# Two chunks' scores in one visit, and both halves of a group's decay and rate projections in one visit

## The chip, the cores and the metric

The kernel runs on one core of a Trainium2 chip. The metric is the device time of one execution in microseconds (us), the median of several runs. TensorE (PE) does the matmuls, VectorE (DVE) and ScalarE (ACT) the elementwise work and the emptying of PSUM banks, GpSimd (POOL) a few fills, and SyncE (SP) starts the transfers.

## The reference, cut to what matters

One layer of a hybrid decoder over 256 tokens with a model width of 2048:

```
z   = rms_norm(x) @ w_in                        # pool part, r, k, v, decay, rate, gate parts
w   = -softplus(-(w0 + tanh(zw) @ w_up)) - 0.5  # decay = exp(-exp(w))
a   = sigmoid(a0 + za @ a_up)                   # rate
kk  = normalise(k * k_k); k = k * (1 + (a - 1) * k_a)
y   = wkv7_scan(r, decay, k, v, -kk, kk * a)    # per head: S = S*w + (S a) b + v k ; y = S r
x   = x + concat(pool_mixer(z), group_norm(y) * gate) @ w_out
x   = x + squared_relu(rms_norm(x) @ w_ffn_up) @ w_ffn_down
x   = x + sigmoid(rms_norm(x) @ w_ple_gate) * (p @ w_ple_proj) ; final rms_norm
```

The scan runs in 16 heads of size 64. The kernel does it in chunks of 64 tokens: within a chunk the step-by-step recurrence becomes products of small matrices, and only the state goes from chunk to chunk.

## The kernel before, in words

**Products in split precision.** Weights come from memory by SP in pieces of 128 x 1024 (`load_raw`). Each is split into a rounded half and a rest: ACT makes `wh` (line 151, two instructions) and DVE makes `wl` (line 152). Three buffers each hold raw, wh and wl. A product is three matmuls: wh by the high half of the activations, wh by the low half, wl by the high half. `gemm_cols` (lines 164 to 166, weights stationary, 256 columns) makes zk, zr and zv; `gemm_toks` (lines 173 to 175, 512 columns) makes the pool part zp and the output products. Both are generators: after each three matmuls they yield their estimated time, 0.36 or 0.68 us.

**The order on PE** is written out by hand: PE keeps the order of the program text. The long products stand in `queue` and are the filler. `fill(us)` takes steps from the queue until their yields sum up to us, and `finish(gen)` takes all that is left of one product. Between the fills stand the short, dependent steps of the recurrence, here called visits. The order on DVE, ACT and SP is set by a scheduler from priorities: the weight splits and several small steps have a high one. A second generator, `inverse`, is advanced beside the filler by `pace`: one step for each 1.65 us of filler in group 0, 0.95 in group 1.

**Two groups of eight heads** (gi = 0, 1) go through the same visits, one after the other. `rwkv_lora(gi)` (line 460) computes decay and rate of 512 channels: the decay rows stand in partitions 0 to 63, the rate rows in 64 to 127, so that two matmuls on 64 rows each can stand beside each other. It goes in two halves of two blocks, with `fill(0.7)` between; a half takes two PSUM banks, lw and la, and ACT empties them with a sigmoid each (lines 463, 464). `rwkv_k` normalises k: eight tiny matmuls into kkn (line 493), a square root, a transpose into rnT, a split into rnp (ACT line 156, DVE line 157), and the broadcast rnb (lines 512, 513), whose second matmul reads the DVE half. `rwkv_r` finishes AR. `rwkv_scores(gi)` (line 572) multiplies BK by AR for four chunks: a chunk takes two banks, one for the even and one for the odd head of each pair, eight matmuls in two passes each, and DVE empties each bank with the causal mask into SC (line 579). Ahead of every chunk but the first stands `fill(2.6)`. `rwkv_sources` scales BK on ACT (line 591) and transposes it (bkt, line 597). `inverse` inverts the triangular blocks: copies of SC into tmp (line 612), a transpose into AT (line 616), 31 pairs of DVE operations on X and tmp (lines 621, 625), and transposes of X into T1G (line 630) and tmp (line 634). `rwkv_merge` (gm, line 649; qm, line 656), `rwkv_values` (vt, bsum) and `rwkv_core` use the results.

**Banks.** Eight PSUM banks: four (`mm`) for the long products and four (`rw`) for all visits. `rw_bank` takes the next one; who takes a bank waits until its last reader is through. Which of the four it is comes out when the program is built.

The order of calls: lora, k and r of group 0, its scores, its inverse beside sources 0, lora 1, k 1 and r 1, then values 0, scores 1, merge 0, and so on. The filler is zk and zr of group 0, zv 0 around the scores of group 0, zk and zr of group 1, zp 0 around the scores of group 1, then zv 1, zp 1 and the output products.

Of the kernel before, what the change touches and what calls it, by code (L numbers as in the profile page):

```python
# [12 lines left out]
ALU = mybir.AluOpType  # L13
# [3 lines left out]
T = 256  # L17
# [23 lines left out]
def trunk(  # L41
# [19 lines left out]
    nc = tc.nc  # L61
# [11 lines left out]
    def rw_bank(name):  # L73
        return psr.tile([128, 512], F32, tag="rw", name=name)
# [5 lines left out]
    def col(name, j):  # L80
        o = PARAM_COLS[name] + j
        return par_sb[:, o : o + 1]
# [142 lines left out]
    def advance():  # L225
        try:
            us = next(queue[0])
            pace(us)
            return us
        except StopIteration:  # L230
            queue.pop(0)
            return 0.0

    def fill(us):

        while us > 0 and queue:
            us -= advance()
# [44 lines left out]
    def e4(tag):  # L282
        return rp.tile([128, 4, T], F32, tag=tag, name=f"{tag}_t")
# [55 lines left out]
    for kg, (tg, n) in enumerate((("tE", 1), ("tF", 2), ("zk", 3), ("zr", 3), ("zv", 3), ("BK", 2), ("BKt", 2))):  # L339
# [13 lines left out]
        if kg == 4:  # L353
            for tt in range(2):
                for i, q in enumerate((2, 3)):
                    nc.tensor.matmul(
                        sbank[:, tt : tt + 1], sums[q][:, 0, tt * 128 : (tt + 1) * 128], ones[:, 0:1],
                        start=i == 0 and tt == 0, stop=i == 1, skip_group_check=True,
# [27 lines left out]
    zwa, zg, zg2 = zf[:, 0], zf[:, 1], zf[0:64, 2]  # L386
# [61 lines left out]
    def rwkv_lora(gi):  # L448
        raw = rp.tile([128, 512], F32, tag="tF", name=f"wa{gi}")
        nc.sync.dma_start(raw, wa_up[:, gi * 512 : (gi + 1) * 512])  # L450
        st = {}
        sg, aa = e4("tA"), e4("tD")
        for half in range(2):
            if half:
                fill(0.7)
            bw, ba = rw_bank("lw"), rw_bank("la")
            for bk, r in ((bw, slice(0, 64)), (ba, slice(64, 128))):
                for j in range(2):
                    pc_ = slice((half * 2 + j) * 128, (half * 2 + j + 1) * 128)
                    nc.tensor.matmul(bk[:, j * T : (j + 1) * T], raw[r, pc_], zwa[r], start=j == 0, stop=True, skip_group_check=True)  # L460
            for j in range(2):
                p = half * 2 + j
                nc.scalar.activation(sg[:, p, :], bw[:, j * T : (j + 1) * T], AF.Sigmoid, bias=col("w0", 4 * gi + p))
                nc.scalar.activation(aa[:, p, :], ba[:, j * T : (j + 1) * T], AF.Sigmoid, bias=col("a0", 4 * gi + p))
        cs = e4("tB")
        for p in range(4):
            nc.vector.tensor_tensor_scan(cs[:, p, :], rmask, sg[:, p, :], 0.0, op0=ALU.mult, op1=ALU.add)
        P, EI = e4("tA"), e4("tC")
        nc.scalar.activation(P, cs, AF.Exp, scale=-WDEC)
        nc.scalar.activation(EI, cs, AF.Exp, scale=WDEC)  # L470
        pc = rp.tile([128, 4, 4], F32, tag="pc", bufs=2, name=f"pc{gi}")
        nc.vector.tensor_copy(pc, P.rearrange("p a (c t) -> p a c t", t=64)[:, :, :, 63])
        st.update(P=P, EI=EI, aa=aa, pc=pc)
        return st
# [84 lines left out]
    def rwkv_scores(gi, st, cs=(0, 1, 2, 3)):  # L559

        AR, BK = st["AR"], st["BK"]
        if 0 in cs:
            st["SC"] = rp.tile([128, 2, 4, 8, 64], F32, tag="SC", bufs=2, name=f"SC{gi}")
        SC = st["SC"]
        cm = cmask.rearrange("s (k t) -> s k t", k=2)
        for c in cs:
            if c:
                fill(2.6)
            bks = [rw_bank(f"sc{e}") for e in range(2)]
            for p in range(4):  # L570
                for e in range(2):
                    nc.tensor.matmul(
                        bks[e][:, p * 128 : (p + 1) * 128],
                        BK[e * 64 : (e + 1) * 64, p, c].rearrange("p i t -> p (i t)"),
                        AR[e * 64 : (e + 1) * 64, p, c].rearrange("p i t -> p (i t)"),
                        start=True, stop=True,
                    )
            for e in range(2):
                nc.vector.tensor_tensor(
                    SC[:, :, c].rearrange("s k (p e) t -> s k p e t", e=2)[:, :, :, e, :],  # L580
                    bks[e].rearrange("s (p k t) -> s k p t", k=2, t=64),
                    cm.unsqueeze(2).to_broadcast([128, 2, 4, 64]), op=ALU.mult,
                )

    def rwkv_sources(gi, st):

# [304 lines left out]
    wag_out()  # L891
    fill(14.0)
    st0 = rwkv_lora(0)
    finish(p_zk0)
    make_bands()
    rwkv_k(0, st0, zk0[0])
    finish(p_zr0)
    rwkv_r(0, st0, zr0[0])
    fill(7.0)
    rwkv_scores(0, st0)  # L900
    beside += [inverse(0, st0), 1.65, 0.0]
    rwkv_sources(0, st0)
    finish(p_zv0)
    st1 = rwkv_lora(1)
    finish(p_zk1)
    rwkv_k(1, st1, zk1[0])
# [4 lines left out]
    rwkv_values(0, st0, zv0[0])  # L911
    fill(7.0)
    rwkv_scores(1, st1)
    rwkv_merge(0, st0)
    beside += [inverse(1, st1), 0.95, 0.0]
# [439 lines left out]
```

## Time and profile before

| | |
|---|---|
| Median of 3 runs | 1205.03 us (1204.11 to 1207.36) |
| Span of the profiled execution, first to last instruction | 1198.9 us |
| Median less that span (what lies around it, and the difference between executions) | 6.1 us |
| TensorE busy | 1179.6 us |
| Mean granted TensorE clock | 0.996 |

The profile is of one execution. Of this execution the page gives the span alone, so a sum is made against 1198.9 us and carried over to the median. A row of the timeline gives start, duration, engine, line, operation, output and inputs; xN means that N equal records are merged. Matmuls overlap, so the distance between two starts, and not the duration, is what one costs. A matmul on plain float32 leaves two records (two passes), one on the split halves leaves one; transposes leave one.

### The profile page before, as it was taken

How to read it: one execution, taken by the hardware profiler on the slowest of the kernel's cores; microseconds unless marked ns; L12 is line 12 of the kernel's file. 1: busy time of each engine (PE TensorE's matmuls, PEld its weight loads, DVE VectorE, ACT ScalarE, POOL GpSimd, SP SyncE). 2: the span in 40 equal slices, each digit the busy share in tenths (PEclk: the TensorE clock that was granted, in tenths of full speed). 3: DMA queues.
4: the chain of work that ended last, by engine and by line, in shares of the span. 5: the costliest groups of instructions: out<-in, count | busy, mean ns of one | idle time of the engine just before them, and what ended most of it. 6: DMA issues, size and time to landing. Idle time of an engine off the chain costs nothing.

```text
span 1198.9 us, 18442 instructions
## 1 busy us (share of the span) xinstructions
PE 1179.6 (98%) x7076; PEld 1013.6 (85%) x7076; DVE 868.1 (72%) x1150; ACT 687.7 (57%) x1260; POOL 15.4 (1%) x65
## 2 busy tenths in 40 slices
PE   8999999999999999999999999999999999999996
PEld 6999988988888888888888788888888888778886
DVE  8687987854556667666888878666667888887552
ACT  6857565665545556555555555555555655668544
POOL 4000000000000000000000000000000000000000
PEclk9999999999999999999999999999999999999999
DMA  7463542354355565666665666665565655776631
GB/s 250 151 202 110 173 155 95 121 186 142 116 177 169 185 185 191 192 193 189 194 203 197 197 197 203 195 187 189 192 193 178 211 198 191 290 234 219 194 121 71
DMA packets 60328, 216.88 MB, mean 181 GB/s; under 512 B 6736, under 2 KB 7120, under 8 KB 59856
## 3 DMA queue, kind: packets, MB, share of 16 engines
q1 hardware_dynamic: 59952, 215.19, 55.1%
q8 instruction: 55, 0.90, 0.3%
q10 hardware_dynamic: 288, 0.52, 0.1%
q14 instruction: 33, 0.27, 0.1%
HBM read 213.59 MB, written 2.10 MB: 180 GB/s over the span
## 4 chain that ended last, share of the span: by engine, by line
PE 81%; DMA 6%; DVE 6%; ACT 4%; issue 2%; SPq 0%; ACTq 0%; DVEq 0%
PE u_w L986 20%; PE u_w L990 10%; DMA raw_d<-in_w_ffn_down_dram 5%; PE d_b L1101 4%; PE d_b L1100 4%; PE d_b L1102 4%; PE gt_b L173 2%; PE gt_b L175 2%; PE gt_b L174 2%; PE zv_b L164 1%; PE zp_b L173 1%; PE wag_b L333 1%; PE zv_b L165 1%; PE zv_b L166 1%; PE zp_b L175 1%
## 5 line engine op out<-in xcount | busy, mean ns | idle before, releaser
L986 PE MATMUL u_w<-h,wh_u 128*128 128x512 f32 x1024 | 355.4, 393 | 0.0
L990 PE MATMUL u_w<-h,wl_u 128*128 128x256 f32 x1024 | 285.5, 279 | 0.0
L151 ACT ACTIVATE wh_u<-raw_u 128x512 fp32r<-128x512 f32 x256 | 147.6, 624 | 162.9 <-PE u_w L986 82.0
L152 DVE TENSOR_TENSOR wl_u<-raw_u,wh_u 128x1024 fp32r<-128x1024 f32 x128 | 156.6, 1224 | 112.1 <-ACT wh_u L151 112.1
L986 PEld LDWEIGHTS u_w<-h,wh_u 128*128 128x128 f32 x1024 | 191.8, 187 | 43.2
L990 PEld LDWEIGHTS u_w<-h,wl_u 128*128 128x128 f32 x1024 | 193.1, 189 | 0.1
L152 DVE TENSOR_TENSOR wl_gt<-raw_gt,wh_gt 128x1024 fp32r<-128x1024 f32 x24 | 29.4, 1225 | 23.9 <-ACT wh_gt L151 23.9
L151 ACT ACTIVATE wh_gt<-raw_gt 128x512 fp32r<-128x512 f32 x48 | 27.8, 631 | 23.0 <-PE gt_b L175 20.4
L1140 DVE TENSOR_TENSOR td<-raw_d 128x512 f32<-128x512 f32 x22 | 15.2, 692 | 33.9 <-DMA raw_d<-in_w_ffn_down_dram 33.9
L164 PE MATMUL zv_b<-hTh,wh_zv 128*128 128x256 f32 x128 | 37.7, 294 | 0.0
L173 PE MATMUL gt_b<-wh_gt,h 128*128 128x512 f32 x96 | 37.5, 390 | 0.0
L164 PE MATMUL zr_b<-hTh,wh_zr 128*128 128x256 f32 x128 | 37.5, 293 | 0.0
L175 PE MATMUL gt_b<-wh_gt,h 128*128 128x512 f32 x96 | 37.4, 389 | 0.0
L174 PE MATMUL gt_b<-wl_gt,h 128*128 128x512 f32 x96 | 37.4, 389 | 0.0
L166 PE MATMUL zr_b<-hTh,wl_zr 128*128 128x256 f32 x128 | 37.2, 290 | 0.1
L164 PE MATMUL zk_b<-hTh,wh_zk 128*128 128x256 f32 x128 | 37.0, 289 | 0.0
L165 PE MATMUL zr_b<-hTl,wh_zr 128*128 128x256 f32 x128 | 36.9, 288 | 0.0
L165 PE MATMUL zk_b<-hTl,wh_zk 128*128 128x256 f32 x128 | 36.3, 284 | 0.5 <-DVE hTl L157 0.5
L166 PE MATMUL zk_b<-hTh,wl_zk 128*128 128x256 f32 x128 | 36.3, 284 | 0.2 <-DVE wl_zk L152 0.2
L166 PE MATMUL zv_b<-hTh,wl_zv 128*128 128x256 f32 x128 | 36.2, 283 | 0.0
L165 PE MATMUL zv_b<-hTl,wh_zv 128*128 128x256 f32 x128 | 36.2, 283 | 0.0
L156 ACT ACTIVATE wad<-raw_d 128x512 fp32r<-128x512 f32 x22 | 13.9, 632 | 36.6 <-DMA raw_d<-in_w_ffn_down_dram 34.5
(804 smaller groups left out, 3081.4 us busy)
## 6 DMA issues: line engine op xcount, KB each, us to landing
raw_u<-in_w_ffn_up_dram SPq DMA_DIRECT2D x128, 512.0 KB, 3.5
raw_d<-in_w_ffn_down_dram SPq DMA_DIRECT2D x128, 512.0 KB, 4.2
raw_gt<-in_w_ple_gate_dram SPq DMA_DIRECT2D x24, 512.0 KB, 3.5
raw_zk<-in_w_in_dram SPq DMA_DIRECT2D x16, 512.0 KB, 3.3
raw_zr<-in_w_in_dram SPq DMA_DIRECT2D x16, 512.0 KB, 3.3
raw_zv<-in_w_in_dram SPq DMA_DIRECT2D x16, 512.0 KB, 3.3
raw_zp<-in_w_in_dram SPq DMA_DIRECT2D x16, 512.0 KB, 3.2
raw_o<-in_w_out_dram SPq DMA_DIRECT2D x16, 512.0 KB, 3.5
```

Source lines behind the costliest of these rows:

```text
L151: nc.scalar.activation(wh[:, a * 512 : (a + 1) * 512], raw[:, a * 512 : (a + 1) * 512], AF.Copy)
L152: nc.vector.tensor_tensor(wl, raw, wh.bitcast(F32), op=ALU.subtract)
L164: nc.tensor.matmul(o, w_h, ah, start=first and ct % 2 == 0, stop=False, skip_group_check=True)
L165: nc.tensor.matmul(o, w_h, al, start=False, stop=False, skip_group_check=True)
L166: nc.tensor.matmul(o, w_l, ah, start=False, stop=last, skip_group_check=True)
L173: nc.tensor.matmul(o, a_h, wh[:, 0:n], start=first, stop=False)
L174: nc.tensor.matmul(o, a_h, wl[:, 0:n], start=False, stop=False)
L175: nc.tensor.matmul(o, a_l, wh[:, 0:n], start=False, stop=last)
L986: nc.tensor.matmul(bank[:, ct, :].rearrange("p (s t) -> p s t", s=2), wh[:, c], hl, start=k == 0, stop=False, skip_group_check=True,)
L990: nc.tensor.matmul(bank[:, ct, 0:T], wl[:, c], hl[:, 0, :], start=False, stop=k == 15, skip_group_check=True)
L1100: nc.tensor.matmul(banks[n], ah, wh, start=first, stop=False)
L1101: nc.tensor.matmul(banks[n], ah, wl, start=False, stop=False)
```

## The change

In `rwkv_lora` both halves take their banks at once and all eight matmuls stand together, decay and rate alternating; the fill between the halves is gone. In `rwkv_scores` two chunks take four banks, their sixteen matmuls stand together, and the four evictions follow. Of the three fills of 2.6 one fill of 5.2 is left. Lines from there on have a number that is two to three higher.

```diff
         sg, aa = e4("tA"), e4("tD")
+        banks = [(rw_bank("lw"), rw_bank("la")) for _ in range(2)]
+        for p in range(4):
+            for bk, r in zip(banks[p // 2], (slice(0, 64), slice(64, 128))):
+                nc.tensor.matmul(
+                    bk[:, p % 2 * T : (p % 2 + 1) * T], raw[r, p * 128 : (p + 1) * 128], zwa[r],
+                    start=p % 2 == 0, stop=True, skip_group_check=True,
+                )
         for half in range(2):
-            if half:
-                fill(0.7)
-            bw, ba = rw_bank("lw"), rw_bank("la")
-            for bk, r in ((bw, slice(0, 64)), (ba, slice(64, 128))):
-                for j in range(2):
-                    pc_ = slice((half * 2 + j) * 128, (half * 2 + j + 1) * 128)
-                    nc.tensor.matmul(bk[:, j * T : (j + 1) * T], raw[r, pc_], zwa[r], start=j == 0, stop=True, skip_group_check=True)
+            bw, ba = banks[half]
             for j in range(2):
...
-        for c in cs:
-            if c:
-                fill(2.6)
-            bks = [rw_bank(f"sc{e}") for e in range(2)]
-            for p in range(4):
+        for c0 in cs[::2]:
+            if c0:
+                fill(5.2)
+            two = [(c, [rw_bank(f"sc{e}") for e in range(2)]) for c in (c0, c0 + 1)]
+            for c, bks in two:
+                for p in range(4):
+                    for e in range(2):
+                        nc.tensor.matmul(
+                            bks[e][:, p * 128 : (p + 1) * 128],
+                            BK[e * 64 : (e + 1) * 64, p, c].rearrange("p i t -> p (i t)"),
+                            AR[e * 64 : (e + 1) * 64, p, c].rearrange("p i t -> p (i t)"),
+                            start=True, stop=True,
+                        )
+            for c, bks in two:
                 for e in range(2):
-                    nc.tensor.matmul(
-                        bks[e][:, p * 128 : (p + 1) * 128],
-                        BK[e * 64 : (e + 1) * 64, p, c].rearrange("p i t -> p (i t)"),
-                        AR[e * 64 : (e + 1) * 64, p, c].rearrange("p i t -> p (i t)"),
-                        start=True, stop=True,
+                    nc.vector.tensor_tensor(
+                        SC[:, :, c].rearrange("s k (p e) t -> s k p e t", e=2)[:, :, :, e, :],
+                        bks[e].rearrange("s (p k t) -> s k p t", k=2, t=64),
+                        cm.unsqueeze(2).to_broadcast([128, 2, 4, 64]), op=ALU.mult,
                     )
-            for e in range(2):
-                nc.vector.tensor_tensor(
-                    SC[:, :, c].rearrange("s k (p e) t -> s k p e t", e=2)[:, :, :, e, :],
-                    bks[e].rearrange("s (p k t) -> s k p t", k=2, t=64),
-                    cm.unsqueeze(2).to_broadcast([128, 2, 4, 64]), op=ALU.mult,
-                )
```

## The prediction on record

> **What bounds the kernel now.** I read the page first, then the busy time by stretches, then the timeline of each engine around the edited visits.
>
> ```profile
> span 1198.9 us, 18442 instructions
> ...
> PE 1179.6 (98%) x7076; PEld 1013.6 (85%) x7076; DVE 868.1 (72%) x1150; ACT 687.7 (57%) x1260; POOL 15.4 (1%) x65
> ...
> PE 81%; DMA 6%; DVE 6%; ACT 4%; issue 2%; SPq 0%; ACTq 0%; DVEq 0%
> ```
>
> TensorE (PE) is busy for 98% of the span and has 81% of the chain that ended last, so PE time saved or lost is time of the kernel, unless another engine sets the pace where it falls. The edits lie between 42 and 190 us. The stretches there (us, then busy time and count of PE, PEld, DVE, ACT, POOL, granted clock, DMA share, GB/s):
>
> ```profile
> 80.00:106.00 26.00, 26.00 (x241) 24.98 (x240) 18.71 (x22) 15.54 (x32) 0.00 (x0) 1.00 0.41 144
> 106.00:118.00 12.00, 12.00 (x97) 11.01 (x96) 11.48 (x30) 10.49 (x20) 0.00 (x0) 1.00 0.29 99
> 118.00:165.00 47.00, 46.65 (x366) 45.21 (x364) 45.97 (x84) 27.87 (x53) 1.10 (x2) 0.96 0.49 168
> 165.00:190.00 25.00, 25.00 (x206) 20.04 (x205) 15.98 (x22) 14.20 (x30) 0.00 (x0) 1.00 0.38 126
> ```
>
> PE is full in all four, but from 106 to 165 us VectorE (DVE) is full too (11.48 of 12, 45.97 of 47): there a PE that comes earlier meets halves of weights that DVE hasn't made yet. The waits of PE between 38 and 420 us are two, both on DVE, none on a DMA:
>
> ```profile
> PE h2t L1007 <- DVE x L945: 0.4, 1, 0.4
> PE zk_b L166 <- DVE wl_zk L152: 0.2, 1, 0.2
> ```
>
> So the loads that change place in SP's list (raw_zp1_3 and raw_zp1_4 behind pool weights and gate rows, the second pool load ahead of x and raw_o1a_4) cost nothing: no PE wait there ends with a transfer. If that cover went, a PE step would wait for the one load that was passed.
>
> **What a visit costs.** Score visit and rate visit of group 0, on PE (start, us):
>
> ```profile
> 85.08 0.28 PE L166 MATMUL zv_b<-hTh,wl_zv 128*128 128x256 f32 x1
> 85.29 1.16 PE L572 MATMUL sc<-AR,BK 64*128 64x128 f32 x16
> 86.38 0.38 PE L164 MATMUL zv_b<-hTh,wh_zv 128*128 128x256 f32 x1
> 86.60 0.28 PE L165 MATMUL zv_b<-hTl,wh_zv 128*128 128x256 f32 x1
> ```
>
> ```profile
> 42.77 0.28 PE L166 MATMUL zk_b<-hTh,wl_zk 128*128 128x256 f32 x1
> 42.98 0.48 PE L460 MATMUL lw<-zf,wa 64*128 64x256 f32 x1
> ...
> 43.30 0.38 PE L460 MATMUL lw<-zf,wa 64*128 64x256 f32 x1
> ...
> 43.52 0.38 PE L460 MATMUL lw<-zf,wa 64*128 64x256 f32 x1
> ...
> 44.05 0.39 PE L164 MATMUL zk_b<-hTh,wh_zk 128*128 128x256 f32 x1
> 44.28 0.28 PE L165 MATMUL zk_b<-hTl,wh_zk 128*128 128x256 f32 x1
> ```
>
> Filling matmuls follow each other every 0.12 us. The 16 passes of a score visit run as 8 pairs (two row halves), one each (1.16 - 0.27) / 8 = 0.11 us. From 85.08 to 86.60 are 1.52 us; less two filler steps (0.24) and 8 pairs (0.88) 0.40 us are left for going in and out. The rate visit gives the same: 44.28 - 42.77 = 1.51, less 0.24, less 4 pairs of 0.22 (43.30 to 43.52): 0.39. lw and la already run side by side before the change (the la rows stand 0.01 us behind), so their new order adds nothing.
>
> **What goes.** Each call of rwkv_lora loses one visit, each of rwkv_scores two: six visits x 0.40 = **2.4 us** less, 1.6 of it ahead of the second scores, 0.8 in them. Nothing else goes: matmuls, evictions and splits are the same in number. The filler isn't kept inside the scores: three fills of 2.6 were 24 steps (zv) and 12 (zp), one of 5.2 is 15 and 8. The other 9 and 4 steps run later under finish; as work nothing is lost, but the second half of the scores stands 9 x 0.36 + 0.8 = 4.0 us earlier in group 0.
>
> At the first rate visit the fourth bank is freed by this DVE row, at 43.98:
>
> ```profile
> 43.50 0.48 DVE L298 SCALAR_TENSOR_TENSOR zf<-wagT,par_sb,zf 128x255 f32<-128x255 f32 x1
> ```
>
> The new visit reaches it at 42.98 + 0.32 + 3 x 0.22 = 43.96: at most 0.1 us, taken as 0.
>
> **What comes: banks.** In the built program the four score tiles of group 0 get banks 4, 7, 6, 5, and no one waits. Group 0's second visit comes 15 x 0.36 = 5.4 us after the first and needs four evictions, 2 x 1.29 = 2.6 us. ACT scales eight pieces of BK in a row instead of four ahead of the next weight's copy; PE asks for that weight only behind the second visit, so this costs nothing while the fill lasts. In group 1 bank 5 is left out: the first visit gets 4, 7, 6, 4 and the second 7, 6, 4, 7. So in each the odd bank of the second chunk is the even bank of the first, and PE must wait inside the visit until DVE has evicted it. Before, the same reuse fell behind a fill. The rows of group 1:
>
> ```profile
> 172.83 1.16 PE L572 MATMUL sc<-AR,BK 64*128 64x128 f32 x16
> ```
>
> ```profile
> 172.13 1.23 DVE L152 TENSOR_TENSOR wl_zp<-raw_zp,wh_zp 128x1024 fp32r<-128x1024 f32 x1 [1.21 <-ACT wh_zp L151]
> 174.03 1.29 DVE L579 TENSOR_TENSOR SC<-sc,cmask 128x512 f32<-128x512 f32 x2 [0.67 <-PE sc L572]
> ```
>
> DVE starts 1.20 us after the visit and evicts two banks in 1.29, the first in some 0.69: ready 1.9 us after the start. PE would want it after 8 pairs and the way in, 1.0 us. That is 0.95 us, and some 0.15 for a pair that is torn: 1.1 us, twice: **+2.2 us**. Behind PE's waiting matmul stand the rest of the chunk, the filler and, the second time, the merge's matmuls; the merge's banks come free while PE finishes the chunk. Bounds: 0.8 (torn pair free) to 2.3 (the split of 1.23 us right ahead of the eviction) a wait. I take 1.1, since DVE is idle for 0.67 us ahead of the eviction, as the row says.
>
> [...] It holds 0.08 of the forecast's chance below, at 1207.6, inside its bounds.
>
> **What comes: DVE's order.** The scheduler sets a new list on DVE and ACT:
>
> ```profile
> 98.96 1.29 DVE L579 TENSOR_TENSOR SC<-sc,cmask 128x512 f32<-128x512 f32 x2 [0.23 <-PE sc L572]
> 102.42 1.23 DVE L152 TENSOR_TENSOR wl_zk<-raw_zk,wh_zk 128x1024 fp32r<-128x1024 f32 x1 [2.17 <-ACT wh_zk L151]
> 103.56 2.16 DVE L616 STREAM_TRANSPOSE AT<-tmp 64x1024 f32<-64x1024 f32 x1
> ...
> 145.84 2.09 DVE L630 STREAM_TRANSPOSE T1G<-X 32x512 f32<-32x512 f32 x2
> 147.78 0.40 DVE L157 TENSOR_TENSOR rnp<-rnT,rnp 8x256 fp32r<-8x256 f32 x1
> 148.10 1.20 DVE L152 TENSOR_TENSOR wl_zr<-raw_zr,wh_zr 128x1024 fp32r<-128x1024 f32 x1
> 149.23 1.15 DVE L634 STREAM_TRANSPOSE tmp<-X 64x512 f32<-64x512 f32 x1
> ```
>
> The inverse of group 0 begins at AT, 3.3 us after the last eviction (100.25). That eviction comes 3.7 us earlier (4.0, less 0.3 that four in a row queue), so AT starts near 99.9, with the same ACT steps between. From AT to the end of rnp, the small split that PE needs for rnb, DVE has 44.6 us without a gap (103.56 to 148.18). In the new list that stretch holds four more operations: one wl_zk that stood ahead of AT, one wl_zr and both transposes of X into tmp, 1.1 + 1.1 + 2 x 1.1 = 4.4 us. So rnp ends at 99.9 + 44.6 + 4.4 = 148.9, where it ended at 148.18. PE used it here:
>
> ```profile
> 148.60 0.38 PE L512 MATMUL rnb<-rnp,hsel 8*128 8x256 f32 x1
> 148.82 0.28 PE L513 MATMUL rnb<-rnp,hsel 8*128 8x256 f32 x1
> ```
>
> With 1.6 us saved PE would come at 147.2 and waits until 148.95 or so. **The 1.6 us are lost again, with 0.2 on top: +1.8.** The waits on wl_zk (122.14 in the row below) lie inside this bound and aren't added. After rnb DVE is ahead of before, as the moved work is done, and the rest is PE's. Bounds: 0 (PE keeps its gain) to 4.4 (AT isn't earlier).
>
> Sum: -2.4 + 2.2 + 1.8 = **+1.6 us**, on the profiled 1198.9 us of span: 1200.5. The median of the runs shown, 1205.03, holds 6.1 us more than that span; I carry the difference over: **1206.6**. About 0.3% (3.6 us) is what a measurement of this kernel can tell from no change.
>
> **The rivals.**
>
> *The gain arrives (faster).* The page's clock is below full here, and PE waits twice:
>
> ```profile
> 122.14 0.38 PE L166 MATMUL zk_b<-hTh,wl_zk 128*128 128x256 f32 x1 [0.23 <-DVE wl_zk L152]
> ```
>
> ```profile
> 142.00:144.00 2.00, 2.00 (x12) 2.00 (x11) 1.90 (x9) 1.95 (x5) 0.00 (x0) 0.52 0.66 240
> 144.00:146.00 2.00, 2.00 (x13) 2.00 (x13) 1.90 (x6) 0.07 (x1) 0.00 (x0) 0.63 0.84 242
> ```
>
> If the earlier inverse lets DVE run ahead, 0.4 us of wait and the dip, 2 x 0.48 + 2 x 0.37 = 1.7 us, go as well, and if DVE empties the banks in time the waits go too: -2.4 - 0.4 - 1.7 = -4.5: 1200.5. Against it: 44.6 us of DVE without a gap.
>
> *Only the banks cost:* -2.4 + 2.2: 1204.8.
>
> *DVE's list comes late (slower).* Place: rnp ahead of rnb. The list is 4.4 us longer and is saved by AT's earlier start alone. If ACT's copies into tmp, now on both sides of a weight split, keep AT later than some 102 us, rnp ends past 151 and PE loses 2.1 us or more besides: price up to 3.7, 1206.6 + 2.1 to 3.7 = 1208.7 to 1210.3, taken as 1209.3.
>
> *Another dip of the clock.* The dip above follows a stretch of tiny matmuls (kkn) and a wait. The new waits make more of these: 1.7 us each, 1208.3. [...]
>
> That the change doesn't do what it says holds for the filler, as counted above; it is in the sum.
>
> **How the numbers follow.** Forecast 0.33 (1205.0 to 1208.2 by its bounds, within 0.3% but for 0.03); only banks 0.10, within; gain arrives 0.17, 0.15 of it faster; late list 0.30, all slower; another dip 0.10, 0.07 of it slower. Faster 0.15, within 0.3% 0.45, slower 0.40. The range leaves out most of the gain's case and the far end of the late list: 1202.0 to 1210.3.
>
> **What would show it.** PE steps of over 0.9 us between sc rows in both visits near 173 and 180 us, none in group 0's; the four evictions in a row; AT near 100; rnp ending near 149 behind two tmp transposes, with PE waiting at the second rnb matmul; PE at scores of group 1 not earlier than 172.8. Wrong, if PE stands at kkn or rnb over 1.5 us later than before, or if group 1's visits run through, or if the clock dips at another place.

## The result, and the profile after

| | before | after |
|---|---|---|
| Median, 22 runs each | 1204.4 us | 1208.88 us |
| Span of the profiled execution | 1198.9 us | 1203.4 us |
| Lost to the granted clock: (1 - mean clock) x span, mean over the runs | 4.1 to 4.3 us (three sets of 35 runs, those of the experiments) | 7.1 us (22 runs) |

The ratio is 1.0029, 95% interval 1.0018 to 1.0040: 3.5 us slower (2.2 to 4.8), about the 0.3% that the prediction took as the least that can be told from no change. (The medians lie 4.5 us apart and the means 3.8, both inside the interval.) The predicted time of 1206.6 is 2.3 us below the median, which lies in the range of 1202.0 to 1210.3; the predicted difference of +1.6 us lies below the interval. In a second set of runs the changed kernel came out at 1.0046 (1.0030 to 1.0061). One run of the variant g1_single, at 1964.1 us and a granted clock of 0.556, is left out of all its figures below.

The page of the changed kernel, its span, the busy time of the engines and the chain that ended last:

```profile
span 1203.4 us, 18444 instructions
...
PE 1182.7 (98%) x7076; PEld 1017.2 (85%) x7076; DVE 869.0 (72%) x1150; ACT 688.9 (57%) x1260; POOL 15.2 (1%) x65
...
PE 87%; DVE 5%; DMA 4%; ACT 3%; issue 1%; SPq 0%; DVEq 0%; ACTq 0%
```

PE has as many matmuls as before and 3.1 us more of busy time, so the loss isn't idle time alone. The waits of PE from 38 to 420 us (line, tile, what it waited for: us in total, times, longest) show the idle part:

```profile
PE sc L574 <- DVE SC L582: 1.1, 2, 0.6
PE zk_b L166 <- DVE wl_zk L152: 1.0, 2, 0.6
PE kkn L494 <- ACT tF_t L482: 0.4, 1, 0.4
PE h2t L1010 <- DVE x L948: 0.4, 1, 0.4
PE rnb L514 <- DVE rnp L157: 0.3, 1, 0.3
```

Before, this list held h2t with 0.4 and wl_zk with 0.2. Every new wait stands at or behind an edited visit; but the 0.3 at rnb, near 65 us, is also in two executions below whose code up to there is the old one (g1_scores_alone and g1_again, 0.3 each), so it can't be put down to the change. The two score visits of group 1 on PE's timeline:

```profile
173.46 1.38 PE L574 MATMUL sc<-AR,BK 64*128 64x128 f32 x18
175.39 1.16 PE L574 MATMUL sc<-AR,BK 64*128 64x128 f32 x14 [0.56 <-DVE SC L582]
...
182.14 1.38 PE L574 MATMUL sc<-AR,BK 64*128 64x128 f32 x18
184.08 1.16 PE L574 MATMUL sc<-AR,BK 64*128 64x128 f32 x14 [0.56 <-DVE SC L582]
185.16 2.38 PE L652 MATMUL gm<-T1G,SC 32*32 32x32 f32 x64
```

Each is torn after its first chunk and one pair: 3.09 us from 173.46 to the end of the second row. Group 0's evictions and the start of its inverse on DVE:

```profile
87.04 2.48 DVE L582 TENSOR_TENSOR SC<-sc,cmask 128x512 f32<-128x512 f32 x4 [0.18 <-PE sc L574]
...
94.66 2.48 DVE L582 TENSOR_TENSOR SC<-sc,cmask 128x512 f32<-128x512 f32 x4
99.30 1.23 DVE L152 TENSOR_TENSOR wl_zv<-raw_zv,wh_zv 128x1024 fp32r<-128x1024 f32 x1 [2.17 <-ACT wh_zv L151]
100.44 2.17 DVE L619 STREAM_TRANSPOSE AT<-tmp 64x1024 f32<-64x1024 f32 x1
```

Four evictions in a row, no wait of PE there, and AT at 100.4 where it was 103.6. The same list ahead of rnb, then PE at it:

```profile
144.62 1.05 DVE L637 STREAM_TRANSPOSE tmp<-X 64x512 f32<-64x512 f32 x1
145.57 1.17 DVE L152 TENSOR_TENSOR wl_zr<-raw_zr,wh_zr 128x1024 fp32r<-128x1024 f32 x1
146.67 1.22 DVE L637 STREAM_TRANSPOSE tmp<-X 64x512 f32<-64x512 f32 x1
147.80 1.17 DVE L152 TENSOR_TENSOR wl_zr<-raw_zr,wh_zr 128x1024 fp32r<-128x1024 f32 x1
148.90 0.40 DVE L157 TENSOR_TENSOR rnp<-rnT,rnp 8x256 fp32r<-8x256 f32 x1
```

```profile
149.17 0.38 PE L513 MATMUL rnb<-rnp,hsel 8*128 8x256 f32 x1
149.39 0.34 PE L514 MATMUL rnb<-rnp,hsel 8*128 8x256 f32 x1
```

Both transposes into tmp now stand ahead of rnp, which ends at 149.3. The last new thing is the clock, in busy time by stretches (the granted clock is the third number from the right):

```profile
142.00:144.00 2.00, 2.00 (x13) 2.00 (x13) 1.97 (x5) 1.69 (x5) 0.00 (x0) 0.66 0.64 238
144.00:146.00 2.00, 2.00 (x12) 2.00 (x11) 2.00 (x4) 0.48 (x1) 0.00 (x0) 0.50 0.46 174
186.00:188.00 2.00, 2.00 (x45) 1.91 (x42) 0.36 (x1) 1.00 (x2) 0.00 (x0) 0.75 0.03 8
188.00:190.00 2.00, 2.00 (x6) 1.54 (x5) 0.00 (x0) 1.98 (x4) 0.00 (x0) 0.50 0.00 0
```

The dip at 142 was there before; the one from 187.0 to 190.4, right behind the second torn visit, is new. In it PE counts as busy throughout (2.00 of 2.00), so this dip shows in the clock column alone. (Every trace of this study, before and after, also ends at half the clock, for its last 4 to 7 us, 6.0 in the trace after; such ends aren't called dips here.)

**Where the time goes, in this pair of executions.** Start of the first instruction of a visit on PE, and the difference less the 0.30 us that the execution after already stands behind at 19 us:

| | before | after | difference less 0.30 | between the rows |
|---|---|---|---|---|
| group 0: lw | 42.98 | 43.28 | 0.00 | |
| kkn | 56.94 | 57.08 | -0.16 | one rate visit less: -0.16 |
| scores | 85.29 | 85.84 | +0.25 | waits near 59 and 65 us: +0.41 |
| group 1: lw | 107.56 | 107.33 | -0.53 | two score visits less: -0.78 |
| values (vt) | 161.72 | 162.34 | +0.32 | one rate visit less, -0.41; waits at wl_zk and kkn: +1.26 |
| merge (gm) | 186.04 | 185.16 | -1.18, or +1.58 for equal work | 12 filler matmuls fewer by then, 2.76; two visits less and two waits: +1.26 |
| h2t | 355.23 | 358.45 | +2.92 | the second dip: +1.34 |

For the other traces below a place is told in the same way: the difference from the trace of before, less what the trace stands behind it at 19 us.

From h2t on the two traces can't be compared, since PE itself runs the same matmuls of the FFN's up product at two speeds, at a granted clock of 1.00. The matmuls of that product from 400 to 570 us (duration: least, median, most), before and after:

```profile
L986 PE MATMUL u_w<-h,wh_u x491: 390/391/392, 399.7 to 569.6; 128*128 128x512 f32 x164
```

```profile
L989 PE MATMUL u_w<-h,wh_u x482: 395/398/404, 399.8 to 569.7; 128*128 128x512 f32 x161
```

The speed doesn't go with the kernel. Of the fourteen traces of this study six have 391 ns here, the changed kernel's second one (changed_again) among them, and eight have 398, the kernel before with one buffer moved among them; the trace after has 391 ns itself from 744 to 900 us. The whole up product takes 524.3 us in the trace of before, 526.9 in the trace after, and up to 532.2 in the others. So these 2.7 us of the difference between the spans are no effect of the change; the 2.9 us up to h2t fit the 3.5 of the ratio.

### The profile page after: what moved, and what is told of

Read it like the earlier page. It is cut to its first block, busy times and chain, and to the rows that moved or that the text cites. A ratio compares the mean times of both kernels' runs of the same rounds, so it can differ in the third digit from the quotient of the medians.

```text
span 1203.4 us, 18444 instructions
## 1 busy us (share of the span) xinstructions
PE 1182.7 (98%) x7076; PEld 1017.2 (85%) x7076; DVE 869.0 (72%) x1150; ACT 688.9 (57%) x1260; POOL 15.2 (1%) x65
## 4 chain that ended last, share of the span: by engine, by line
PE 87%; DVE 5%; DMA 4%; ACT 3%; issue 1%; SPq 0%; DVEq 0%; ACTq 0%
PE u_w L989 20%; PE u_w L993 10%; PE d_b L1104 6%; PE d_b L1105 6%; PE d_b L1103 6%; PE gt_b L173 2%; PE gt_b L175 2%; PE gt_b L174 2%; DMA raw_d<-in_w_ffn_down_dram 1%; PE zp_b L173 1%; PE zv_b L164 1%; DMA graw<-in_w_ple_gate_dram 1%; PE d_w L1104 1%; PE d_w L1105 1%; PE d_w L1103 1%; PE zv_b L166 1%
## 5 line engine op out<-in xcount | busy, mean ns | idle before, releaser
L152 DVE TENSOR_TENSOR wl_zp<-raw_zp,wh_zp 128x1024 fp32r<-128x1024 f32 x16 | 19.5, 1221 | 16.1 <-ACT wh_zp L151 16.1
```

The lines of the kernel that those rows point to most:

```text
L152: nc.vector.tensor_tensor(wl, raw, wh.bitcast(F32), op=ALU.subtract)
```

## The experiments

The theory: visits saved and DVE's list cancel, the banks cost 2.1 us, and the torn visits bring a second dip of the clock, which the sum had left out. Time is read from the ratio to the kernel before, run beside the variant on the same chip (three chips in all), places from the trace, and the clock from all runs of a kernel:

| kernel | ratio (95%) | lost to the clock, us |
|---|---|---|
| before | 1 | 4.3, 4.1, 4.2 |
| changed | 1.0029 (1.0018 to 1.0040) | 7.1 |
| changed_again | 1.0046 (1.0030 to 1.0061) | 7.5 |
| bank_freed | 0.9994 (0.9980 to 1.0008) | 5.1 |
| g1_scores_alone | 1.0003 (0.9988 to 1.0017) | 5.4 |
| g1_again (the same kernel) | 1.0024 (1.0003 to 1.0045) | 5.3 |
| g1_freed | 1.0010 (0.9994 to 1.0025) | 3.9 |
| g0_scores_alone | 1.0006 (0.9987 to 1.0024) | 4.6 |
| lora_alone | 0.9984 (0.9968 to 1.0000) | 4.6 |
| t1g_moved_in_before | 0.9995 (0.9980 to 1.0011) | 3.7 |
| g1_single | 1.0022 (1.0001 to 1.0043) | 5.0 |
| gap_before_merge | 1.0038 (1.0019 to 1.0057) | 5.4 |
| freed_later | 1.0008 (0.9993 to 1.0023) | 5.1 |
| no_pairs | 1.0010 (0.9993 to 1.0028) | 5.2 |

The means in the last column are uncertain by 0.2 to 0.7 us (their standard error; 0.1 to 0.2 for before), so that 3.7 and 4.6 hardly differ. One dip of 3.41 us counts as 1.71 in the last column and costs 1.5: in a dip a filler matmul takes 0.213 us instead of 0.12 (zr in the trace of before, 142.19 to 145.18 us against 138.31 to 139.15), so 16 are done in place of 28.

**The bank.** Bank 5 is left out of group 1's scores since it holds the first values product until ACT copies it into UV (line 673); UV takes the buffer of T1G, which the merge has to read first. ACT's row in the trace after shows that this copy waits for the merge's second product:

```profile
193.40 1.21 ACT L673 ACTIVATE UV<-vt 64x512 f32<-64x512 f32 x2 [0.49 <-PE qm L659]
```

It comes behind all scores. With T1G elsewhere the bank is free in time:

```diff
-        T1G = rp.tile([64, 32, 32], F32, tag=tags[0], name=f"T1G{gi}")
+        T1G = rp.tile([64, 32, 32], F32, tag=tags[0] if gi else "q3", name=f"T1G{gi}")
```

> The changed kernel, in which the matrix T1G of group 0 lies in another buffer, so that the first values bank (bank 5) is emptied before the scores of group 1 and these get four different banks (5, 4, 7, 6 in each visit). Theory: the two score visits of group 1 shrink from 3.02 us to 2.0 (-2.1 us), and with the waits goes the second dip of the clock that the changed kernel shows at 187.0 to 190.4 us (-1.5): 3.6 us less than the changed kernel, within 0.5 us of the kernel before. Rival: the dip belongs to the small matmuls of the merge behind the visits: it stays, and 2.1 us less than the changed kernel, some 1.4 us more than before. Second rival: VectorE's four evictions themselves set the pace of the visits (the merge then waits for its banks): less than 1 us is gained.

The score visits and the merge on PE, and the stretches around them:

```profile
173.49 2.06 PE L574 MATMUL sc<-AR,BK 64*128 64x128 f32 x32
...
181.14 2.06 PE L574 MATMUL sc<-AR,BK 64*128 64x128 f32 x32
183.13 2.21 PE L652 MATMUL gm<-T1G,SC 32*32 32x32 f32 x64
```

```profile
165.00:190.00 25.00, 25.00 (x262) 20.65 (x261) 16.26 (x22) 15.55 (x32) 0.00 (x0) 1.00 0.32 106
...
186.00:188.00 2.00, 2.00 (x22) 1.43 (x22) 0.00 (x0) 2.00 (x3) 0.00 (x0) 1.00 0.00 0
188.00:190.00 2.00, 2.00 (x56) 1.92 (x54) 1.89 (x2) 1.95 (x4) 0.00 (x0) 1.00 0.00 0
```

Each visit runs through in 2.06 us instead of 3.09: 2 x 1.03 us, the predicted 2.2. The clock is 1.00 in all these stretches; the dip at 142 us is in this trace too. At h2t PE is 3.7 us earlier than in the changed kernel (-0.78 against +2.92), and the whole loss is gone: 0.9994. Over the runs the clock loses 5.1 us in place of 7.1 to 7.5, and 4.3 in the kernel before. The theory holds; the rival (a dip that stays) and the second rival (evictions as the bound) fall. That the buffer by itself brings nothing is shown by the kernel before with the same edit:

> The kernel before, in which T1G of group 0 lies in the other buffer too, nothing else. It tells whether the other buffer by itself brings something. Theory: nothing, since no score visit of the kernel before waits for a bank: TensorE at the merge within 0.2 us of the kernel before. Rival: the earlier emptying of the values bank helps by itself, and 1 us or more is gained at the merge.

0.9995. Its values and merge stand 1.05 us earlier than in the trace of before, but 0.5 of it is there at group 0's scores, far ahead of the buffer's use, and this execution had no dip at 142 us; from the values to the merge nothing changes. This trace brought something else. The two longest of PE's waits from 38 to 420 us:

```profile
PE rym L707 <- DVE sbd L747: 0.8, 1, 0.8
PE rnb L513 <- DVE rnp L157: 0.7, 1, 0.7
```

Without a dip ahead of it, PE waits 0.7 us for rnp even with nothing joined; g1_scores_alone, g1_again and g1_freed, whose code is the old one up to there, show the same 0.7. The trace of before hid this: its dip at 142 us held PE back. (Why rym, behind the merge, waits 0.8 us here isn't known; at h2t PE stands at +0.07.)

**Group 1's scores alone, with and without the bank.** The kernel before with `cs` taken in twos for gi = 1 only:

```diff
-        for c in cs:
-            if c:
-                fill(2.6)
+        n = 2 if gi else 1
+        for c0 in cs[::n]:
+            if c0:
+                fill(2.6 * n)
```

> The kernel before, in which the scores of group 1 alone go in double visits, with the one fill of 5.2 us; group 0 and the projections are as before. Theory: this part alone brings the loss: -0.8 us of two visits, +2.1 us of waiting inside the double visits, +1.5 us of a second dip of the clock near 187 us: +2.8 us against the kernel before by the trace behind the merge. Rival: the dip comes only with the other parts: +1.3 us.

> Once more the kernel before with double visits for the scores of group 1 alone, beside its variant with the freed bank on one chip. Theory: from the values to the merge 1.25 us lost, the clock loses some 1 to 2.5 us more than in the kernel before: 0.2% slower. Rival, by the first reading of this kernel (1.0003): the loss isn't there unless the other parts are.

> The kernel before with double visits for the scores of group 1 alone, and with T1G of group 0 in the other buffer, so that these visits get four banks. Theory: two visits less and no wait: 0.8 us won from the values to the merge, the clock as in the kernel before; all other work unchanged: 0.05 to 0.1% faster than before, at the edge of what shows in the median. Rival: the four evictions in a row make the merge late, and nothing is won.

From the values to the merge PE loses 1.26 us in both executions of the first kernel (with the 2.76 us of filler that it has done less by then), as in the changed one. Behind it the first execution has a dip of four times 3.41 us, from 188.2 to 201.9, the second one dip at 190:

```profile
188.00:190.00 2.00, 2.00 (x32) 1.84 (x30) 0.00 (x0) 1.15 (x2) 0.00 (x0) 0.55 0.00 0
190.00:192.00 2.00, 2.00 (x6) 1.55 (x5) 0.00 (x0) 1.98 (x4) 0.00 (x0) 0.50 0.00 0
...
196.00:200.00 4.00, 4.00 (x27) 3.35 (x26) 1.64 (x8) 1.81 (x4) 0.00 (x0) 0.50 0.05 16
```

So the dip belongs to this part, and how long it lasts changes from one execution to the next. Over the runs it costs 1.1 us of clock more than before, less than the single traces let one expect. In time the two readings, 1.0003 and 1.0024, overlap, and the expected 0.2% lies just outside the first. With the bank freed the same visits last 2.06 us each, 0.81 us are won from the values to the merge, as expected, and the clock loses 3.9 us, as before. In the median 0.8 us can't be seen (1.0010, 0.9994 to 1.0025).

**The other parts alone.** Group 0's scores in double visits (n = 1 if gi else 2), and the joined projections with the scores as before:

> The kernel before, in which the scores of group 0 alone go in double visits. Theory: 0.8 us are saved at the scores (86 to 101 us), no wait inside the visits; the inverse starts some 3 us earlier, two transposes into tmp go ahead of rnp, and waits on wl_zk, kkn or rnp between 117 and 149 us give back the gain: TensorE at the values (161.7 us before) within 0.3 us of before. Rival: VectorE is early enough and the 0.8 us arrive at the values.

> The kernel before, in which only the projections of decay and rate go in one visit a group. Theory: in group 0 0.2 us are saved and lost again on rnp near 65 us; in group 1 0.4 us are saved at 108 us and lost again on wl_zk, kkn or rnp, since VectorE is full from 106 to 148 us: TensorE at the values within 0.3 us of before. Rival: the 0.6 us stay saved.

The main waits of PE in the first, then in the second:

```profile
PE rnb L513 <- DVE rnp L157: 1.7, 2, 1.4
PE zk_b L166 <- DVE wl_zk L152: 0.6, 1, 0.6
...
PE kkn L493 <- ACT tF_t L481: 0.4, 1, 0.4
```

```profile
PE rnb L514 <- DVE rnp L157: 0.9, 2, 0.7
PE zk_b L166 <- DVE wl_zk L152: 0.5, 1, 0.5
```

The visits are saved (-0.78 us between the scores and group 1's lw in the first; -0.34 at group 0's kkn in the second) and lost again. At the values PE is 1.76 and 0.98 us later than in the trace of before, more than the 0.3 expected. But in both the dip comes at 152 us, behind rnb, where it was ahead of rnb in before. The fair comparison is with the four executions whose code is the old one up to the values (two with T1G in the other buffer): t1g_moved_in_before and g1_scores_alone, without a dip there, and g1_again and g1_freed, with the dip at 152 us. From group 1's lw to the values, with the 1.5 us of their own dip taken off, these four change by -0.54 to -0.57 us against the trace of before, group 0's scores alone by +0.89 and the projections alone by -0.57. So group 0's scores lose 1.4 us there, their own 0.8 and 0.6 to 0.7 more, and the projections lose just the 0.4 that their visit saved. The rivals (the gain stays) fall in the trace; the ratios, 1.0006 and 0.9984, are too wide to add to it, and the second would even allow the gain.

**Is it DVE's list?** The changed kernel without the 31 pairs of group 0's inverse:

```diff
-        for k in range(31):
+        for k in range(31 if gi else 0):
```

> The changed kernel, in which group 0's inverse leaves out its 31 pairs of operations on VectorE (the result of the recurrence is then another), so that VectorE has some 17 us of slack between 102 and 142 us. Theory: the gain of the visits is lost to VectorE's list alone, so the waits on wl_zk, on kkn's input and on rnp between 117 and 149 us go, and TensorE at the values is 0.9 to 1.3 us earlier than in the changed kernel. Rival: kkn's wait hangs on ScalarE's order and stays: 0.2 us less. Second rival: the waits on wl_zk end with a transfer or with ScalarE and stay: less than 0.3 us is gained.

```profile
PE zk_b L166 <- DVE wl_zk L152: 1.3, 2, 0.7
PE sc L574 <- DVE SC L582: 1.1, 2, 0.6
PE h2t L1010 <- DVE x L948: 0.4, 1, 0.4
```

The waits at kkn and rnb are gone, and with them the dip between 140 and 160 us. At the values PE stands at -2.35 us, 2.7 us earlier than in the trace after. Of that the missing dip is 1.5, and 0.9 stand there already at group 0's scores, ahead of the pairs, so this pair of traces can't price the list. changed_again can: it stands within 0.1 us of this trace at the scores and has its dip behind rnb. With that dip's 1.5 us taken off, PE is 1.7 us earlier here, more than the 0.9 to 1.3 expected; the waits at kkn and rnb are 1.8 us shorter and those at wl_zk 0.4 longer. So the pairs on DVE are what takes the gain back at kkn and rnb. That the 1.6 us saved arrive in full isn't shown: PE is 1.3 to 1.8 us ahead of t1g_moved_in_before and g1_scores_alone, but without the pairs these too might lose their 0.7 us of wait at rnb, and the kernel before without the pairs was not run. The wait at wl_zk stays. It can't be settled here, since ACT's list changed too: its copies from tmp to SC, 2.1 us at 108 us, now stand ahead of the emptying of zv.

**Can the visits be moved behind the list?** With the bank freed, 1.1 us more filler ahead of kkn and of rnb:

```diff
-        fill(5.4)
+        fill(6.5)
...
-        fill(1.8)
+        fill(2.9)
```

> The changed kernel with the freed bank, and with 1.1 us more of filler ahead of kkn and ahead of rnb in both groups (fill 6.5 for 5.4, 2.9 for 1.8). Theory: the waits for tF (kkn) and for rnp (rnb), 0.8 us in all with the one near 65 us, go, since VectorE and ScalarE get 1.1 and 2.2 us more: TensorE at the values 0.5 to 0.9 us earlier than with the freed bank alone; what follows rnb (AR, BK, the scores) isn't late. Rival: VectorE's list is late as a whole, and the wait appears again at the scores or on a weight half.

The theory fell, and the rival is right: the wait appears again, on a weight half. PE in group 0, then the ACT row that decides it:

```profile
59.02 0.39 PE L166 MATMUL zr_b<-hTh,wl_zr 128*128 128x256 f32 x1 [1.88 <-DVE wl_zr L152]
```

```profile
55.89 1.30 ACT L482 ACTIVATE tF_t<-zk_t,par_sb 128x256 f32<-128x256 f32 x3
57.09 1.66 ACT L151 ACTIVATE wh_zr<-raw_zr 128x512 fp32r<-128x512 f32 x3
```

The added filler needs a weight that ACT makes only after the squares for kkn. PE runs out of weights for 1.9 us, and the clock is at half for two times 3.41 us right behind (60.4 to 67.2). The ratio is 1.0008, no better than with the bank alone.

**The second dip.** The changed kernel once more, with group 1's scores as before, and with filler between the scores and the merge (`fill(2.6)` ahead of `rwkv_merge(0, st0)`):

> The changed kernel itself once more, beside the variants on one chip. Theory: 0.2 to 0.4% slower than the kernel before, with 2 to 3 us more lost to the granted clock over its runs. If the second dip is an accident of one execution, its runs lose no more to the clock than those of the kernel before.

> The changed kernel, in which the scores of group 1 go chunk by chunk as before. Theory: without the waits for banks and the clock lost behind them, 1.3 us by the trace from the values to the merge and some 2.5 us of clock are won back: 4.3 to 5.1 us lost to the granted clock a run, within 0.15% of the kernel before. Rival: the clock is lost to the joined projections or to group 0's scores: 7 us lost to the clock as in the changed kernel, 0.3% slower.

> The changed kernel with 2.6 us of filler between group 1's last scores and the merge. Theory: the waits for banks stay (two of about 1 us), but the stretch of 3.4 us that holds a wait no longer holds the merge's tiny matmuls too: the clock loses 1.5 to 2.5 us less a run than in the changed kernel (some 5 in place of 7.2), 0.1 to 0.2% slower than before. Rival: the wait inside a visit is enough by itself: the clock loses as much as in the changed kernel.

The changed kernel's loss is there in the second set of runs, in time and in clock (7.5 us). Its trace this time waits 1.4 us at rnb, and the dip behind the merge lasts from 187.3 to 201.0:

```profile
PE rnb L514 <- DVE rnp L157: 1.4, 1, 1.4
```

```profile
186.00:188.00 2.00, 2.00 (x57) 2.00 (x57) 1.16 (x2) 0.59 (x1) 0.00 (x0) 0.84 0.22 80
188.00:190.00 2.00, 2.00 (x16) 1.68 (x14) 0.00 (x0) 1.28 (x2) 0.00 (x0) 0.50 0.00 0
```

Without group 1's double visits the clock loses 5.0 us, with the gap 5.4, and neither trace has a dip between 160 us and the end. With the gap both waits are still there (1.1 us in all), so a wait by itself isn't enough. All traces together say more: in all five in which group 1's double visits wait for a bank and the merge follows at once (after, changed_again, g1_scores_alone, g1_again, no_pairs) a dip follows; in none of the other nine is there one at the merge. The 3.41 us ahead of these five dips, a stretch as long as one dip, held 43 to 64 of the merge's tiny matmuls, 14 to 16 score passes, at most one filler matmul, and 0.06 to 0.56 us of wait. In two of them (g1_again, no_pairs) nearly all of the wait lay earlier. So in these traces the dip goes with the torn visit and the merge close together, and not with a certain length of wait ahead of it; why the clock falls was not shown.

In time both missed. g1_single gave 1.0022 where 0.15% at most was expected, with an interval from nothing to the changed kernel's loss; its trace, with the dip at 143 us as in before, stands at +0.16 at the merge and +0.18 at h2t, as the theory has it. The gap gave 1.0038 for 0.1 to 0.2%, no faster than the changed kernel. These two show the clock's share by the clock, not by the time.

## Why the prediction came out as it did

- **Visits, -2.4 us: right.** -0.16, -0.78, -0.41 and -0.81 (the last from g1_freed) are 2.16 us. The short one is group 0's rate visit, with its last two blocks out of step; in changed_again it gave 0.41.
- **Banks, +2.2 us: right in mechanism, place and size.** 2 x 1.03 us, and gone when bank 5 is free. Behind it stood a fact that the prediction had only as a list of banks: bank 5 waits for a buffer, not for an engine.
- **The 0.08 at 1207.6: wrong.** It stood for all four double visits lasting as long as their evictions, an estimate of the author's: 4 x 0.645 = 2.6 us against 1.8 for 16 pairs of 0.11, so 0.8 us over each and +3.2 in place of +2.2. The traces don't agree: with four banks the visits run through in 2.06 us (bank_freed) while DVE still empties them (four in 2.48 us in the trace after, no wait on PE). Here the free banks decide, not the eviction's rate.
- **DVE's order, +1.8 us: right in size, in part right in place.** AT came at 100.4 (99.9 was forecast), rnp ended at 149.3 (148.9), and at the values the loss against the start was 0.32 us (0.2). In this execution 1.0 us of it fell at wl_zk and 0.2 at kkn, and PE came to rnb just as rnp ended, since the dip at 142 us had held it back. That the total at the values agrees in this pair is partly luck, as both traces have that dip. The better test is changed_again against t1g_moved_in_before, both without a dip ahead of rnb: from wl_zk to rnb PE waits 2.7 against 1.0 us (every wait above 0.1 us counted), 1.7 more, of it 0.6 on weight halves, 0.4 at kkn and 0.7 at rnb. The prediction had all of it at rnb.
- **The step that failed: "Another dip of the clock" was left out of the sum.** It stood among the rivals at 0.10 and 1.7 us, though the prediction's own bank waits bring it: it is gone when the bank is free. A dip at another place was also one of the signs by which the prediction was to be wrong. It came in the profiled execution (187.0 to 190.4, 1.34 us by the table of places) and over all runs: 7.1 to 7.5 us lost against 4.1 to 4.3, about 3.1 us, or 3.1 x 1.5 / 1.71 = 2.7 us of time. The sum of +1.6 with it is +4.3; measured were 3.5 (2.2 to 4.8) and, in the second set of runs, 5.5 (3.6 to 7.3).
- **The gain doesn't arrive,** as forecast; without the pairs on DVE PE reaches the values 1.7 us earlier (no_pairs against changed_again).

Open stays what the wait at wl_zk ends with, why the clock falls, and whether the parts together lose more to the clock (3.1 us) than alone (0.3, 0.4 and 1.1, 1.8 in all): the difference of 1.3 has a standard error of some 0.7.

## What to carry to other kernels

Before two visits are joined, look up in the built program which banks they get, and what the missing one waits for: here a buffer that a later visit still had to read decided, and one changed tag gave 3.7 us back. A wait inside a visit that tiny matmuls follow at once can cost more than itself: in all five traces of this kind the clock fell to half right behind it, for at least 3.41 us; price the two together. And where another engine's list had no gap (DVE was busy for 44.90 of the 47 us from 118 to 165), time saved on PE ahead of it was lost again, and PE came 1.7 us earlier once that list was shorter (no_pairs); delaying PE's visit instead only moved the wait to the next weight, 1.88 us in freed_later.

## What the runs showed of the hardware

- In the dips the granted clock was 0.50, for 3.41 us or for several times that. In the profiled execution of the changed kernel they begin at 142.64 and 187.01 us; in changed_again one lasts from 187.34 to 201.0 us, four times 3.41; in freed_later one lasts from 60.4 to 67.2, two times; in g1_freed one lasts from 1080.0 to 1083.4. They stand elsewhere in another execution of the same kernel: the changed kernel has two dips ahead of its end in one trace and five stretches of 3.41 us in another. A single trace can't price them; the mean clock over a dozen runs can. In the 3.41 us ahead of the dip at 187.0 PE idled for 0.48 us and was otherwise busy with score passes and the merge's tiny matmuls; the cause of the dips was not shown.
- A dip was paid in part by a wait. Ahead of a wait for another engine it took the place of that wait (before: dip at 142 us, no wait at rnb; the same code without a dip there: 0.7 us of wait). From group 1's lw to the values the dip of 1.5 us made the trace of before only 0.6 us longer than t1g_moved_in_before, which has none.
- At one granted clock of 1.00 the same 512-column matmul took 391 ns in six executions and 398 in eight, over 170 us, and in the profiled execution of the changed kernel 398 in one stretch and 391 in a later one.
